# A hybrid encoder layer on one core: the seven sums of the second feed-forward product are combined to four blocks by VectorE as they are made, their operands are loaded by SyncE into four buffers, and the residual is kept in column chunks

## The chip, the core and the metric

One core of a Trainium2 chip runs the whole layer in one launch. The metric is the device time of that launch in microseconds (us). Three runs of the kernel before took 2177.72, 2178.38 and 2178.72 us; the median is 2178.38 us.

The engines have short names here: PE multiplies matrices, DVE (VectorE) does elementwise work on two tensors, ACT (ScalarE) does copies, casts and activations, POOL (GpSimd) and SP (SyncE) only issue DMAs in the part that matters. SBUF is the on-chip memory, PSUM the small memory that PE writes its sums to (eight banks of 128 x 512 floats), DRAM the memory off the core.

## What is computed

The input is 512 tokens of 2048 floats. The layer is a mixer (short convolutions beside gated linear attention), then a feed-forward block, each with a residual, and a last RMSNorm. Cut to what matters here:

```python
x = x + concat(y_conv, y_gla) @ w_out                 # 2048 x 2048
h = rmsnorm(x, norm2_g)
x = x + square(relu(h @ w_ff1)) @ w_ff2               # 2048 x 8192, 8192 x 2048
out = rmsnorm(x, norm_f_g)
```

## The kernel before

**Precision.** Every float operand of PE is split in two: `hi`, its value rounded to PE's format (a cast, done by ACT), and `lo`, the rest (a subtraction, done by DVE). A product is three matmuls, hi by hi, hi by lo, lo by hi. `split_w` (L602 to L607) does this for weights; it has three buffers for `hi` and three for `lo`, so that the operands of one product can be made only when the product three earlier is done. `plus` (L609 to L612) adds two weight blocks on DVE.

**Seven products in place of eight.** Both feed-forward products are done on 2 x 2 blocks by Winograd's form of Strassen's method: seven products of sums of blocks. Each is called by a number f (1 to 7), in the order `FORMS = (1, 5, 7, 3, 6, 2, 4)`. From the seven results come the four blocks of the output by seven additions.

**The first feed-forward product** (L615 to L670) makes, in 32 steps g, 256 rows of hidden values, squares them, and stores their seven sums ("forms") to DRAM in `a_keep`. The last two steps store plain blocks in `a_last`.

**The second product** (L681 to L791) is the part that changes. The 8192 hidden rows are cut in four blocks `blk` of two groups `grp`; the 2048 output columns in four column steps `n`. The loops run over blk, n, grp and f. A product is 24 matmuls of 256 columns per group (12 in group 1 of block 3, which is half as deep) and adds into a PSUM bank over the two groups. Names such as `lo_f_0113` say blk 0, n 1, grp 1, f 3. The weights come in quarters `raw_f` of 512 KB (four buffers, SP's queue, L598). Per product, ACT casts `hi_f` (L605) and DVE subtracts `lo_f` (L606); four of the seven also need a `plus` (L611).

The other operand, the forms of hidden values, is loaded in `form` (L683 to L696): seven per group, each 512 KB from `a_keep` into one of two buffers `st`, by a DMA that POOL issues (L688); then a cast `ah` (L694) and a subtraction `al` (L695). A group's forms stay for all four column steps. The next block's forms are made beside the products at the change from one block to the next: in (n, grp) = (3, 1) for group 0 and in (0, 0) for group 1.

When a product's second group is done, `evict` (L712 to L719) copies its bank by ACT to a tile `p` of 256 KB, which POOL stores to DRAM in `p_keep`; from block 1 on the DMA adds to what is there. In block 3 `combine(n)` (L721 to L744) loads the seven sums back by SP (L726), makes the four blocks with seven additions on DVE (L729), and adds them, scaled by the token's norm `r2`, to the residual tiles `x3t` with eight operations of 256 columns (L741). A last short stage multiplies the two plain groups and finishes the output (L838 to L867).

**The residual.** After the mixer, x is held in four tiles `xr` of 128 tokens by 2048. The output projection runs in five column chunks (`out_chunk`, L555; three of 512 columns, two of 256); each adds to its columns of `xr`. When all are done, four DMAs of 1024 KB store `xr` in `x_keep` (L575), from where block 3 loads it. The SBUF of these tiles is used again for the weights' sums `w` and the buffers `st`.

**What sets the order.** The functions are called in the order written, but a scheduler then orders the instructions of each engine by when it takes them to be ready. On the chip each engine keeps that order: what stands behind a waiting instruction waits too.

Of the kernel before, what the change touches and what calls it, by code (L numbers as in the profile page):

```python
# [14 lines left out]
P = 128  # L15
SEQ = 512
D = 2048
# [22 lines left out]
def hymba_kernel(  # L40
# [444 lines left out]
    p_keep = [[tc.dram_tile([P, 2, HALF], F32, name=f"p_keep{n}{f}") for f in FORMS] for n in range(4)]  # L485
# [3 lines left out]
    xs = [res.tile([P, D], F32, name=f"xr_{i}", tag=f"x{i}") for i in range(NT)]  # L489
    for i in range(NT):  # L490
        nc.gpsimd.dma_start(xs[i], x[i * P : (i + 1) * P, :])
# [28 lines left out]
    def h_block(kt, pool):  # L520
        b = bank(f"htr_{kt}", "aux")
        for i in range(NT):
            T.transpose(b[:, i * P : (i + 1) * P], xs[i][:, kt * P : (kt + 1) * P], ident)
# [29 lines left out]
    with tc.tile_pool(name="n2", bufs=1) as n2:  # L553

        def out_chunk(n, c, wsrc, w0, nunit, ncol, ktu, hook, ready=()):  # L555
# [10 lines left out]
        for n in range(3):  # L566
            at = {2: (2 * n - 2,), 5: (2 * n - 1,)} if n else {}
            out_chunk(n, slice(n * 512, (n + 1) * 512), w_out, 8 * n, 8, 512, 2, pairs_at(at), w_ready if n == 0 else ())
        for n in (3, 4):
            c = slice((n + 3) * HALF, (n + 4) * HALF)  # L570
            at = {0: (4,), 1: (5,), 2: (6,)} if n == 4 else {}
            out_chunk(n, c, w_out_tail, 4 * (n - 3), 4, HALF, 4, pairs_at(at))
        h_pair(7, n2)
        for i in range(NT):
            nc.gpsimd.dma_start(x_keep[i], xs[i])  # L575
# [98 lines left out]
    PLACE = {1: 0, 2: 1, 4: 2, 7: 3, 5: 4, 6: 5, 3: 6}  # L674
    first = [(hf, f"h{n}") for n in range(14)]
# [5 lines left out]
    with tc.tile_pool(name="ff", bufs=1, reuse_waits="tile") as ff:  # L681

        def form(blk, grp, f):  # L683

            n = FORMS.index(f)
            m = 2 if (blk, grp) == (3, 1) else 4
            raw = wt.tile([P, 4, HALF], F32, name=f"st_{blk}{grp}{f}", tag="st", bufs=2)
            nc.gpsimd.dma_start(raw[:, :m, :], a_keep[2 * blk + grp][PLACE[f]][:, :m, :])  # L688
# [23 lines left out]
        def evict(blk, n, f, dst):  # L712
            sq = ff.tile([P, 2, HALF], F32, name=f"p_{blk}{n}{f}", tag="sq", bufs=8)
            S.copy(sq, dst.rearrange("p (a b) -> p a b", a=2))  # L714
            keep = p_keep[n][FORMS.index(f)]
            if blk == 0:
                nc.gpsimd.dma_start(keep, sq)
            else:
                nc.gpsimd.dma_start(keep, sq, accum_op=ALU.add)  # L719

        def combine(n):  # L721

            s = {}
            for f in FORMS:
                s[f] = ff.tile([P, 2, HALF], F32, name=f"s_{n}{f}", tag="sq", bufs=8)
                nc.sync.dma_start(s[f], p_keep[n][FORMS.index(f)])  # L726

            def op(out, a, b, kind):
                V.tensor_tensor(out=s[out], in0=s[a], in1=s[b], op=kind)  # L729

            op(6, 6, 1, ALU.subtract)
            op(2, 1, 2, ALU.add)
            op(5, 5, 6, ALU.add)
            op(6, 6, 7, ALU.add)
            op(3, 5, 3, ALU.add)
            op(7, 5, 7, ALU.add)
            op(4, 4, 6, ALU.subtract)
            for f, row, col in ((3, 0, 0), (2, 0, 1), (7, 1, 0), (4, 1, 1)):
                for i in range(2):
                    xc = x3t[2 * row + i][col][:, n, :]  # L740
                    V.scalar_tensor_tensor(  # L741
                        out=xc, in0=s[f][:, i, :], scalar=r2[:, 2 * row + i : 2 * row + i + 1], in1=xc,
                        op0=ALU.mult, op1=ALU.add,
                    )  # L744
# [3 lines left out]
        for f in FORMS:  # L748
            form(0, 0, f)
        for blk in range(4):  # L750
            for n in range(4):
                dst = {f: fbank(f"f2_{blk}{n}{f}") for f in FORMS}
                for grp in range(2):
# [10 lines left out]
                    for f in FORMS:  # L764
                        if f == 5:
                            w = w1 = plus(b11, b12, m * HALF, f"{name}{f}")
                        elif f == 7:
                            w = plus(b11, b21, m * HALF, f"{name}{f}")
                        elif f == 6:
                            w = w3 = plus(w1, b21, m * HALF, f"{name}{f}")  # L770
                        elif f == 4:
                            w = plus(w3, b22, m * HALF, f"{name}{f}")
                        else:
                            w = {1: b12, 3: b21, 2: b22}[f]
                        product2(blk, grp, f, w, m, dst[f], f"{name}{f}")
                        if grp == 1:
                            evict(blk, n, f, dst[f])
# [4 lines left out]
                if blk == 3:  # L782
                    if n == 0:
                        x3t = []
                        for i in range(NT):
# [156 lines left out]
```

## Time and profile before

| | |
|---|---|
| median of three runs | 2178.38 us |
| the profiled execution | 2175.88 us, of which 2173.9 us span from first to last instruction |
| PE busy | 2089.0 us, 14408 matmuls |
| DVE busy | 1437.5 us |
| ACT busy | 933.8 us |
| POOL busy | 162.0 us |
| moved by DMA | 323.91 MB, 149 GB/s in the mean |

The profile divides the span by engine and instruction. A "group" is all instructions of a line with the same names and shapes; "idle before" is how long the engine stood before them, and for whom. A "wait" row names the waiting engine and who ended the wait. A row of "windows" gives, for a stretch of the span, each engine's busy time with its count of instructions (x), then the granted share of PE's clock (PEclk, 1.00 is full) and of DMA. PE's busy time is modelled and runs on over short pauses, so the count of matmuls in a stretch says more than the busy time. The first product ends at about 1434 us, the second at about 2114 us.

### The profile page before, as it was taken

What the parts mean: (1) busy time and instruction counts of PE and PEld (TensorE: products, weight loads), DVE (VectorE), ACT (ScalarE), POOL (GpSimd) and SP (SyncE); (2) the same over time, 40 slices, a digit from 0 to 9 for tenths busy, and PEclk for the clock granted to TensorE, in tenths of its full rate; (3) what the DMA queues carried; (4) which work ended last, traced back from release to release, by engine and by line L of the source; (5) the groups of instructions that cost most, each with busy time, mean ns of one, the idle gap of its engine ahead of it and who ended that gap; (6) DMA issues with size and microseconds to landing.
All of it is one profiled execution on the core that took longest, in us unless ns stands there. A gap on an engine that the chain in (4) does not pass through costs nothing.

```text
span 2173.9 us, 34501 instructions
## 1 busy us (share of the span) xinstructions
PE 2089.0 (96%) x14408; PEld 1935.0 (89%) x14408; DVE 1437.5 (66%) x1680; ACT 933.8 (43%) x1222; POOL 162.0 (7%) x233
## 2 busy tenths in 40 slices
PE   8999999999999989999999999999989989987887
PEld 7988877877888889999999999999989989987885
DVE  4232236656754488888888888887776676665666
ACT  6242212222333345555555555465454454453343
POOL 0000000000000000000000000011111121121120
PEclk9999999999999999999999999999999999999899
DMA  7223322222243344444445444566576786776574
GB/s 294 87 79 97 97 78 87 78 78 80 85 174 92 93 148 158 158 158 158 150 139 168 158 141 149 159 233 198 165 238 141 172 230 158 172 210 197 151 210 138
DMA packets 97532, 323.91 MB, mean 149 GB/s; under 512 B 10901, under 2 KB 10949, under 8 KB 95840
## 3 DMA queue, kind: packets, MB, share of 16 engines
q1 hardware_dynamic: 65088, 222.46, 32.0%
q0 software_dynamic: 32288, 99.24, 16.6%
q8 instruction: 113, 1.85, 0.3%
q14 instruction: 43, 0.35, 0.0%
HBM read 255.34 MB, written 66.32 MB: 148 GB/s over the span
## 4 chain that ended last, share of the span: by engine, by line
PE 73%; issue 15%; DMA 5%; DVE 3%; POOL 3%; ACT 1%; POOLq 0%; ACTq 0%; DVEq 0%; SPq 0%
PE f1c L625 8%; PE f1a L625 8%; PE f L707 8%; PE f1d L625 4%; PE f1e L625 4%; PE f1b L625 4%; DMA st<-a_keep 3%; PE tm_op L75 3%; PE tm_op L76 3%; PE tm_op L77 3%; POOL p_keep L719 2%; PE fm_ch L75 1%; PE fm_cc L75 1%; PE tm_v L76 1%; PE tm_v L75 1%
## 5 line engine op out<-in xcount | busy, mean ns | idle before, releaser
L707 PE MATMUL f<-lo_f,ah 128*128 128x256 f32 x1568 | 452.5, 289 | 43.4 <-DVE lo_f L606 43.4
L707 PE MATMUL f<-hi_f,ah 128*128 128x256 f32 x1568 | 446.9, 286 | 9.0 <-ACT hi_f L605 9.0
L707 PE MATMUL f<-hi_f,al 128*128 128x256 f32 x1568 | 447.1, 285 | 0.0
L606 DVE TENSOR_TENSOR lo_f<-w_f,hi_f 128x1024 fp32r<-128x1024 f32 (+1 forms) x256 | 304.4, 1190 | 149.6 <-ACT hi_f L605 148.3
L605 ACT CAST hi_f<-w_f 128x1024 fp32r<-128x1024 f32 (+1 forms) x256 | 262.0, 1023 | 241.5 <-PE f1c L625 97.0
L707 PEld LDWEIGHTS f<-lo_f,ah 128*128 128x128 f32 x1568 | 303.1, 193 | 50.0 <-DVE lo_f L606 49.9
L707 PEld LDWEIGHTS f<-hi_f,ah 128*128 128x128 f32 x1568 | 302.8, 193 | 10.5 <-ACT hi_f L605 10.4
L707 PEld LDWEIGHTS f<-hi_f,al 128*128 128x128 f32 x1568 | 303.9, 194 | 0.0
L605 ACT CAST hi_f<-raw_f 128x1024 fp32r<-128x1024 f32 (+1 forms) x192 | 196.6, 1024 | 192.1 <-PE f L707 82.9
L606 DVE TENSOR_TENSOR lo_f<-raw_f,hi_f 128x1024 fp32r<-128x1024 f32 (+1 forms) x192 | 227.6, 1186 | 20.9 <-ACT hi_f L605 20.7
L611 DVE TENSOR_TENSOR w_f<-raw_f,raw_f 128x1024 f32<-128x1024 f32 (+1 forms) x128 | 152.1, 1191 | 91.9 <-DMA raw_f<-in_w_ff 84.0
L611 DVE TENSOR_TENSOR w_f<-w_f,raw_f 128x1024 f32<-128x1024 f32 (+1 forms) x128 | 152.4, 1190 | 3.7
L625 PE MATMUL f1c<-Sh,hi_f 128*128 128x256 f32 x512 | 145.0, 283 | 6.2 <-ACT hi_f L605 6.2
L625 PE MATMUL f1c<-Sh,lo_f 128*128 128x256 f32 x512 | 144.9, 283 | 0.4 <-DVE lo_f L606 0.4
L625 PE MATMUL f1c<-Sl,hi_f 128*128 128x256 f32 x512 | 144.6, 282 | 0.0
L625 PE MATMUL f1a<-Sh,hi_f 128*128 128x256 f32 x512 | 144.2, 282 | 0.0
L625 PE MATMUL f1a<-Sh,lo_f 128*128 128x256 f32 x512 | 144.1, 282 | 0.0
L625 PE MATMUL f1a<-Sl,hi_f 128*128 128x256 f32 x512 | 144.0, 281 | 0.0
L75 PE MATMUL tm_op<-hi_op,yh 128*128 128x512 f32 (+1 forms) x304 | 106.2, 349 | 0.0
L714 ACT COPY p<-f 128x512 f32<-128x512 f32 x112 | 65.6, 586 | 92.9 <-PE f L707 92.9
L76 PE MATMUL tm_op<-lo_op,yh 128*128 128x512 f32 (+1 forms) x304 | 105.3, 346 | 0.0
L77 PE MATMUL tm_op<-hi_op,yl 128*128 128x512 f32 (+1 forms) x304 | 105.0, 345 | 0.0
(353 smaller groups left out, 4923.0 us busy)
## 6 DMA issues: line engine op xcount, KB each, us to landing
raw_f<-in_w_ff SPq DMA_DIRECT2D x240, 512.0 KB, 4.0
p_keep<-p POOLq DMA_DIRECT2D x112, 256.0 KB, 5.6
a_keep<-y POOLq DMA_DIRECT2D x30, 896.0 KB, 5.1
st<-a_keep POOLq DMA_DIRECT2D x49, 512.0 KB, 4.6
raw_op<-in_w_out SPq DMA_DIRECT2D x22, 512.0 KB, 3.6
raw_og<-in_w_feat SPq DMA_DIRECT2D x16, 512.0 KB, 3.7
raw_cc<-in_w_feat SPq DMA_DIRECT2D x16, 512.0 KB, 3.8
raw_ch<-in_w_feat SPq DMA_DIRECT2D x16, 512.0 KB, 3.7
```

The costliest lines, as they stand in the source:

```text
L75: T.matmul(dst, l[0], r[0], start=start, stop=False)
L76: T.matmul(dst, l[0], r[1], start=False, stop=False)
L77: T.matmul(dst, l[1], r[0], start=False, stop=stop)
L605: S.copy(hi[:, :n], src)
L606: V.tensor_tensor(out=lo[:, :n], in0=src, in1=hi[:, :n].bitcast(F32), op=ALU.subtract)
L611: V.tensor_tensor(out=w[:, :n], in0=in0, in1=in1, op=ALU.add)
L625: T.matmul(dst[:, :HALF], l[:, c], r, start=start and p == m == 0, stop=p == 7 and m == 2, skip_group_check=True,)
L707: T.matmul(d, l[:, k, t], r[:, c], start=grp == k == i == e == 0, stop=grp == 1 and k == m - 1 and e == 2, skip_group_check=True,)
L714: S.copy(sq, dst.rearrange("p (a b) -> p a b", a=2))
L719: nc.gpsimd.dma_start(keep, sq, accum_op=ALU.add)
```

## The change

1. **The sums stay on the chip.** `evict` no longer copies all seven banks out. Products run in the order `ORDER = (1, 6, 5, 3, 7, 2, 4)`. ACT copies only bank 1 (`q`); DVE reads the other banks and builds the four blocks by seven operations of 128 x 512 per column step (`t`, `x`, `v` and the blocks `c0` to `c3`), each reading one PSUM bank. Only the blocks go to DRAM, in `c_keep`: stored in block 0, added by the DMA in blocks 1 and 2. In block 3 the kept block `s` is loaded by POOL ahead of its step, added on DVE, and the result is added to `x3t` as before; `combine` is gone.
2. **Forms.** `st` is loaded by SP. Every second form of a full group takes one of two more buffers, slots `second[14]` and `second[15]`, which the first product uses up to its last matmuls for its forms 6, 2 and 4.
3. **Weights' sums.** In the new order the sums for f 5 and 6 are both made at f 6.
4. **The residual.** `xr` is 20 tiles, one per chunk and 128 tokens, loaded by 20 DMAs; each is stored in `x_keep` as soon as its chunk is added. The squares for the norm go to PSUM.

The diff, cut:

```diff
+    c_keep = [[tc.dram_tile([P, 2, HALF], F32, name=f"c_keep{n}{q}") for q in range(4)] for n in range(4)]
...
+    for n, c in enumerate(chunks):
+        for i in range(NT):
+            nc.gpsimd.dma_start(xs[n][i], x[i * P : (i + 1) * P, c])
...
             def put(i, b):
-                V.tensor_tensor(out=xs[i][:, c], in0=b[:, :ncol], in1=xs[i][:, c], op=ALU.add)
-                sq = n2.tile([P, 512], F32, name=f"sq2_{n}{i}", tag="sq2", bufs=1)
-                S.activation(sq[:, :ncol], xs[i][:, c], AF.Square, accum_out=ss2[:, i, n : n + 1])
+                xc = xs[n][i]
+                V.tensor_tensor(out=xc, in0=b[:, :ncol], in1=xc, op=ALU.add)
+                sq = bank(f"sq2_{n}{i}", "one")
+                S.activation(sq[:, :ncol], xc, AF.Square, accum_out=ss2[:, i, n : n + 1])
+                nc.gpsimd.dma_start(x_keep[i][:, chunks[n]], xc)
...
-        for i in range(NT):
-            nc.gpsimd.dma_start(x_keep[i], xs[i])
...
+    ORDER = (1, 6, 5, 3, 7, 2, 4)
...
-            raw = wt.tile([P, 4, HALF], F32, name=f"st_{blk}{grp}{f}", tag="st", bufs=2)
-            nc.gpsimd.dma_start(raw[:, :m, :], a_keep[2 * blk + grp][PLACE[f]][:, :m, :])
+            name = f"st_{blk}{grp}{f}"
+            if n % 2 and (blk, grp) != (3, 1):
+                raw = in_slot(second[14 + n // 2 % 2], name, F32)
+            else:
+                raw = wt.tile([P, 4, HALF], F32, name=name, tag="st", bufs=2)
+            nc.sync.dma_start(raw[:, :m, :], a_keep[2 * blk + grp][PLACE[f]][:, :m, :])
...
+        def evict(blk, n, f, dst, had):
+            p = dst[f].rearrange("p (a b) -> p a b", a=2)
+            def value(name, in0, in1, kind, bufs):
+                t = ff.tile([P, 2, HALF], F32, name=f"{name}_{blk}{n}", tag=name[0], bufs=bufs)
+                V.tensor_tensor(out=t, in0=in0, in1=in1, op=kind)
+                return t
+            def block(q, in0, in1, kind):
+                t = value(f"c{q}", in0, in1, kind, 4)
+                if blk == 0:
+                    nc.gpsimd.dma_start(c_keep[n][q], t)
+                elif blk < 3:
+                    nc.gpsimd.dma_start(c_keep[n][q], t, accum_op=ALU.add)
+                else:
+                    V.tensor_tensor(out=t, in0=t, in1=had["s"][q], op=ALU.add)
+                    for i in range(2):
+                        k = q // 2 * 2 + i
+                        xc = x3t[k][q % 2][:, n, :]
+                        V.scalar_tensor_tensor(
+                            out=xc, in0=t[:, i, :], scalar=r2[:, k : k + 1], in1=xc, op0=ALU.mult, op1=ALU.add
+                        )
+            if f == 1:
+                had["q"] = ff.tile([P, 2, HALF], F32, name=f"q_{blk}{n}", tag="q", bufs=1)
+                S.copy(had["q"], p)
+            if f == 6:
+                had["t"] = value("t", p, had["q"], ALU.subtract, 1)
+            if f == 5:
+                had["x"] = value("x", p, had["t"], ALU.add, 1)
+            if f == 3:
+                block(0, p, had["x"], ALU.add)
+            if f == 7:
+                had["v"] = value("v", p, had["t"], ALU.add, 1)
+                block(2, p, had["x"], ALU.add)
+            if f == 2:
+                block(1, p, had["q"], ALU.add)
+            if f == 4:
+                block(3, p, had["v"], ALU.subtract)
...
+                        if f == 6:
+                            w1 = plus(b11, b12, m * HALF, f"{name}5")
+                            w = w3 = plus(w1, b21, m * HALF, f"{name}6")
...
-                    combine(n)
```

Where the instructions stand now, at three places. **First**, DVE at the start of the first product. `w_f_05` is the first `plus` of its step 0, `lo_f_05` the split that its second product waits for; the rows ahead of them belong to the last pair of normed hidden inputs (`d_7`, `Sl`) and to the norm factor `r_`. Before:

```order
L577 TENSOR_REDUCE a_5708<-ss_4161 128x4
L544 TENSOR_TENSOR d_7_5700<-h_5680,d_7_5696 128x256
L531 TENSOR_TENSOR Sl_5665<-d_7_5692,Sh_5664 128x256
L531 TENSOR_TENSOR Sl_5667<-d_7_5696,Sh_5666 128x256
L531 TENSOR_TENSOR Sl_5665<-d_7_5700,Sh_5664 128x256
L118 TENSOR_SCALAR a_5708<-a_5708 128x4
L108 RECIPROCAL r_4162<-r_4162 128x4
```

In the row of before follow six more operations on the norm factor, then three `plus` (`w_f_05`, `w_f_07`, `w_f_06`), then `lo_f_05`. The same place now, with lines of the changed file:

```order
L582 TENSOR_REDUCE a_5744<-ss_4181 128x4
L616 TENSOR_TENSOR w_f_05_5812<-raw_f_01_5770,raw_f_00_5768 128x1024
L537 TENSOR_TENSOR Sl_5705<-d_7_5732,Sh_5704 128x256
L537 TENSOR_TENSOR Sl_5707<-d_7_5736,Sh_5706 128x256
L550 TENSOR_TENSOR d_7_5740<-h_5720,d_7_5736 128x256
L118 TENSOR_SCALAR a_5744<-a_5744 128x4
L616 TENSOR_TENSOR w_f_07_5844<-raw_f_01_5770,raw_f_02_5772 128x1024
L537 TENSOR_TENSOR Sl_5705<-d_7_5740,Sh_5704 128x256
L108 RECIPROCAL r_4182<-r_4182 128x4
L611 TENSOR_TENSOR lo_f_05_5815<-w_f_05_5812,hi_f_05_5814 128x1024
```

`w_f_05` moved up to right behind the reduction, and `lo_f_05` stands ahead of most of the norm's operations and of the third `plus`.

**Second**, a regular column step (blk 0, n 1, grp 1). Before, ACT alternates casts with the copies `p` of finished banks:

```order
L714 COPY p_14105<-f_011_13850 128x512
L605 CAST hi_f_0113_14174<-raw_f_0112_14073 128x1024
L714 COPY p_14138<-f_015_13851 128x512
L605 CAST hi_f_0116_14207<-w_f_0116_14205 128x1024
L714 COPY p_14171<-f_017_13852 128x512
L605 CAST hi_f_0112_14238<-raw_f_0113_14075 128x1024
```

Now DVE has the seven operations that read the banks (L728) between its splits and sums:

```order
L611 TENSOR_TENSOR lo_f_0113_14207<-raw_f_0112_14108,hi_f_0113_14206 128x1024
L728 TENSOR_TENSOR t_14174<-f_016_13886,q_14140 128x512
L611 TENSOR_TENSOR lo_f_0117_14240<-w_f_0117_14237,hi_f_0117_14239 128x1024
L728 TENSOR_TENSOR x_14204<-f_015_13887,t_14174 128x512
L616 TENSOR_TENSOR w_f_0206_14381<-w_f_0205_14379,raw_f_0202_14347 128x1024
L611 TENSOR_TENSOR lo_f_0112_14273<-raw_f_0113_14110,hi_f_0112_14272 128x1024
L728 TENSOR_TENSOR c_01_14234<-f_013_13888,x_14204 128x512
L611 TENSOR_TENSOR lo_f_0114_14306<-w_f_0114_14303,hi_f_0114_14305 128x1024
L616 TENSOR_TENSOR w_f_0207_14467<-raw_f_0201_14345,raw_f_0202_14347 128x1024
L728 TENSOR_TENSOR v_14267<-f_017_13889,t_14174 128x512
L728 TENSOR_TENSOR c_01_14269<-f_017_13889,x_14204 128x512
```

The operation on a bank stands behind the split of a product two further on, so that PE has work while DVE waits for the bank.

**Third**, DVE in block 3, from n 0 to n 1. Before, the additions of `combine(0)` stand inside the next step's first group, behind the split of its fourth product (`s` are the sums that came back from DRAM):

```order
L606 TENSOR_TENSOR lo_f_3107_19556<-w_f_3107_19553,hi_f_3107_19555 128x1024
L611 TENSOR_TENSOR w_f_3104_19669<-w_f_3106_19611,raw_f_3103_19493 128x1024
L606 TENSOR_TENSOR lo_f_3103_19584<-raw_f_3102_19491,hi_f_3103_19583 128x1024
L729 TENSOR_TENSOR s_19459<-s_19459,s_19451 128x512
L729 TENSOR_TENSOR s_19453<-s_19453,s_19459 128x512
```

Five more such additions and the eight operations of L741 follow there, then `lo_f_3106`. Now the last of the four blocks stands ahead of the next step's first split, and more behind it:

```order
L742 SCALAR_TENSOR_TENSOR x_01_19064<-c_30_19462,r_4182,x_01_19064 128x256
L742 SCALAR_TENSOR_TENSOR x_11_19068<-c_30_19462,r_4182,x_11_19068 128x256
L728 TENSOR_TENSOR c_30_19485<-f_304_19062,v_19439 128x512
L611 TENSOR_TENSOR lo_f_3101_19514<-raw_f_3100_19505,hi_f_3101_19513 128x1024
L738 TENSOR_TENSOR c_30_19485<-c_30_19485,s_19085 128x512
L616 TENSOR_TENSOR w_f_3106_19543<-w_f_3105_19541,raw_f_3102_19509 128x1024
L742 SCALAR_TENSOR_TENSOR x_21_19072<-c_30_19485,r_4182,x_21_19072 128x256
L742 SCALAR_TENSOR_TENSOR x_31_19076<-c_30_19485,r_4182,x_31_19076 128x256
L616 TENSOR_TENSOR w_f_3107_19629<-raw_f_3101_19507,raw_f_3102_19509 128x1024
L611 TENSOR_TENSOR lo_f_3106_19546<-w_f_3106_19543,hi_f_3106_19545 128x1024
```

The whole combining of step n is thus ahead of, or among, the first splits of step n + 1, in the row from `t` of step n on: `t`, `lo_f_3013`, `x`, `lo_f_3017`, `lo_f_3012`, `c0`, `lo_f_3014`, an addition L738, `v`, two operations L742, `c2`, `c1`, two additions, and then the rows shown.

More of the change, by code (lines that the diff above doesn't have):

```diff
@@ L484, in hymba_kernel @@
     a_last = tc.dram_tile([2, P, 4, HALF], F32, name="a_last")
-    p_keep = [[tc.dram_tile([P, 2, HALF], F32, name=f"p_keep{n}{f}") for f in FORMS] for n in range(4)]
+    c_keep = [[tc.dram_tile([P, 2, HALF], F32, name=f"c_keep{n}{q}") for q in range(4)] for n in range(4)]
     hf = ctx.enter_context(tc.tile_pool(name="hf", bufs=1))
@@ L488, in hymba_kernel @@
     res = late.enter_context(tc.tile_pool(name="res", bufs=1))
-    xs = [res.tile([P, D], F32, name=f"xr_{i}", tag=f"x{i}") for i in range(NT)]
-    for i in range(NT):
-        nc.gpsimd.dma_start(xs[i], x[i * P : (i + 1) * P, :])
+    chunks = [slice(0, 512), slice(512, 1024), slice(1024, 1536), slice(1536, 1792), slice(1792, 2048)]
+    xs = [
+        [res.tile([P, c.stop - c.start], F32, name=f"xr_{n}{i}", tag=f"x{n}{i}") for i in range(NT)]
+        for n, c in enumerate(chunks)
+    ]
+    for n, c in enumerate(chunks):
+        for i in range(NT):
+            nc.gpsimd.dma_start(xs[n][i], x[i * P : (i + 1) * P, c])
     ss2 = const_tile("ss2", [P, NT, 5])
@@ L710, in product2 @@
                         )
[L712 to L744, printed above, removed]
@@ L746, in hymba_kernel @@
         aforms = {}
         x3t = None
-        for f in FORMS:
+        for f in ORDER:
             form(0, 0, f)
@@ L751, in hymba_kernel @@
             for n in range(4):
-                dst = {f: fbank(f"f2_{blk}{n}{f}") for f in FORMS}
+                dst = {f: fbank(f"f2_{blk}{n}{f}") for f in ORDER}
+                had = {}
+                if blk == 3:
+                    if n == 0:
+                        x3t = []
+                        for i in range(NT):
+                            x3t.append([in_slot(second[7 + 2 * i + c], f"x3_{i}{c}", F32) for c in range(2)])
+                            for c in range(2):
+                                nc.gpsimd.dma_start(
+                                    x3t[i][c], x_keep[i][:, c * 1024 : (c + 1) * 1024].rearrange("p (a b) -> p a b", a=4)
+                                )
+                    had["s"] = []
+                    for q in range(4):
+                        had["s"].append(ff.tile([P, 2, HALF], F32, name=f"s_{n}{q}", tag="s", bufs=4))
+                        nc.gpsimd.dma_start(had["s"][q], c_keep[n][q])
                 for grp in range(2):
@@ L781, in hymba_kernel @@
                             form(blk + 1, 0, f)
[L782 to L785, printed above, removed]
-                            x3t.append([in_slot(second[7 + 2 * i + c], f"x3_{i}{c}", F32) for c in range(2)])
-                            for c in range(2):
-                                nc.gpsimd.dma_start(
-                                    x3t[i][c], x_keep[i][:, c * 1024 : (c + 1) * 1024].rearrange("p (a b) -> p a b", a=4)
-                                )
-                    combine(n)
         slots = first + second[:7]
@@ L849, in hymba_kernel @@
                 )
-                sq = ff.tile([P, 512], F32, name=f"sq3_{n}{i}", tag="sq", bufs=8)
-                S.activation(sq, x3[n], AF.Square, accum_out=ss3[:, i, n : n + 1])
+                sq = ff.tile([P, 2, HALF], F32, name=f"sq3_{n}{i}", tag="c", bufs=4)
+                S.activation(sq.rearrange("p a b -> p (a b)"), x3[n], AF.Square, accum_out=ss3[:, i, n : n + 1])
                 if n < 3:
```

27 lines of the change are left out of this document (11 added, 16 removed).

## The prediction

> **What bounds the kernel now.** I read the page's busy shares first, then the groups of instructions with the idle time ahead of them. From the page:
>
> ```profile
> span 2173.9 us, 34501 instructions
> L707 PE MATMUL f<-lo_f,ah 128*128 128x256 f32 x1568 | 452.5, 289 | 43.4 <-DVE lo_f L606 43.4
> L606 DVE TENSOR_TENSOR lo_f<-w_f,hi_f 128x1024 fp32r<-128x1024 f32 (+1 forms) x256 | 304.4, 1190 | 149.6 <-ACT hi_f L605 148.3
> L714 ACT COPY p<-f 128x512 f32<-128x512 f32 x112 | 65.6, 586 | 92.9 <-PE f L707 92.9
> ```
>
> PE bounds nearly all of it; in the second product it stands before a matmul almost only for a split `lo_f`. A share over the span does not say where, so the third view is the table by windows, cut at the start of the first product, the start of the second, a regular part, the changes of block, the steps of block 3, and the last stage:
>
> ```profile
> core 0: us, PE busy (x) PEld busy (x) DVE busy (x) ACT busy (x) POOL busy (x), PEclk, DMA share, GB/s
> 789.30:800.50 11.20, 4.31 (x17) 3.64 (x17) 10.76 (x23) 4.65 (x8) 0.00 (x0) 0.70 0.84 318
> 1434.00:1480.00 46.00, 41.08 (x339) 40.05 (x338) 39.25 (x35) 29.31 (x35) 9.64 (x18) 1.00 0.77 262
> 1579.00:1630.00 51.00, 44.23 (x340) 43.01 (x339) 38.82 (x34) 28.29 (x32) 9.15 (x17) 0.93 0.71 235
> 1749.00:1820.00 71.00, 63.70 (x509) 61.90 (x508) 51.85 (x45) 38.15 (x45) 16.71 (x23) 0.98 0.81 212
> 1820.00:1919.00 99.00, 99.00 (x840) 98.89 (x840) 69.50 (x58) 46.74 (x53) 15.07 (x19) 1.00 0.67 168
> 1919.00:1988.50 69.50, 57.33 (x423) 54.99 (x422) 40.19 (x43) 32.34 (x45) 19.48 (x28) 0.93 0.75 204
> 1988.50:2032.00 43.50, 33.37 (x254) 32.57 (x253) 27.51 (x38) 14.97 (x21) 6.02 (x7) 0.88 0.63 165
> 2032.00:2075.00 43.00, 33.31 (x255) 32.51 (x254) 28.20 (x38) 14.98 (x21) 6.02 (x7) 0.91 0.63 167
> 2075.00:2114.20 39.20, 33.43 (x254) 32.82 (x254) 29.10 (x39) 17.51 (x24) 6.27 (x8) 0.89 0.70 200
> ```
>
> The row 1820:1919 sets the scale: PE without a pause, 99.00 / 840 = 0.1179 us a matmul, so 24 x 0.1179 = 2.83 us a product and 19.8 us a group of seven. In the other rows the excess is the width less the count times 0.1179: 46.00 - 40.0 = 6.0; 51.00 - 40.1 = 10.9; 71.00 - 60.0 = 11.0; 69.50 - 49.9 = 19.6; block 3: 125.7 - 763 x 0.1179 = 35.7; and at the first product 11.20 - 2.0 = 9.2. Together some 92 us, the most that this change could free. A regular column step has no excess: what is made cheaper there is worth nothing.
>
> **Start of the first product: -2.3.** PE and DVE there, each in its timeline:
>
> ```profile
> 795.54 0.58 PE L625 MATMUL f1c<-Sh,hi_f 128*128 128x256 f32 x1 [6.16 <-ACT hi_f L605]
> 797.87 0.58 PE L625 MATMUL f1c<-Sh,lo_f 128*128 128x256 f32 x1 [0.39 <-DVE lo_f L606]
> ```
>
> ```profile
> 790.12 0.17 DVE L577 TENSOR_REDUCE a<-ss 128x4 f32<-128x20 f32 x1
> 793.18 2.36 DVE L611 TENSOR_TENSOR w_f<-raw_f,raw_f 128x1024 f32<-128x1024 f32 x2
> 796.60 2.35 DVE L606 TENSOR_TENSOR lo_f<-w_f,hi_f 128x1024 fp32r<-128x1024 f32 x2
> ```
>
> PE's second product waits for the cast of `w_f_05`, then for `lo_f_05`. `w_f_05` now stands right behind the reduction, near 790.3 and not 793.18; its split follows cast, two more operations of 1.2 us and a few small ones later, near 794.3 and not 796.60. The gain is 2.3, at most 4 if the cast is the only thing left between, 0 if the early `plus` now waits for its tile.
>
> **Start of the second product: 0.** The forms load four at a time and not two, which alone would free most of the 6.0. But form 6 now is the second product, and its new buffer is held by the last matmuls of the first product. What a form costs is in the rows of DMA issues and, for cast and split, in the groups of a regular stretch (1480 to 1579):
>
> ```profile
> raw_f<-in_w_ff SPq DMA_DIRECT2D x240, 512.0 KB, 4.0
> st<-a_keep POOLq DMA_DIRECT2D x49, 512.0 KB, 4.6
> ...
> x<-x_keep POOLq DMA_DIRECT2D x8, 512.0 KB, 9.4
> ```
>
> ```profile
> L606 DVE TENSOR_TENSOR lo_f<-w_f,hi_f 128x1024 fp32r<-128x1024 f32 x20 | 24.5, 1224 | 16.6 <-ACT hi_f L605 16.6
> L605 ACT CAST hi_f<-w_f 128x1024 fp32r<-128x1024 f32 x19 | 19.9, 1049 | 14.3 <-PE f L707 14.3
> ```
>
> Load 4.6 + cast 1.05 + split 1.22 - 2.83 of product 1 = 4.0 us of pause, and a pause like that lowers the clock, some 1.7 more: 5.7 against 6.0. I take 0; -4 if the matmuls that hold the slot end early, +3 if the load is late behind the first weights on SP's queue.
>
> **Regular column steps: 0.** Per step DVE gains seven operations on banks. The nearest rows are an addition from PSUM in the mixer (L423) and the same addition from SBUF (L729):
>
> ```profile
> L423 DVE TENSOR_TENSOR up<-fm_ch,cc 128x512 f32<-128x512 f32 x8 | 5.5, 692 | 20.3 <-PE fm_ch L77 20.3
> L729 DVE TENSOR_TENSOR s<-s,s 128x512 f32<-128x512 f32 x28 | 17.7, 686 | 14.7 <-DMA s<-p_keep 14.6
> L741 DVE SCALAR_TENSOR_TENSOR x<-s,r,x 128x256 f32<-128x256 f32 x32 | 13.1, 476 | 0.0
> ```
>
> A step is 22 operations of 1.22 and seven of 0.69: 31.7 of 39.6 us. It fits, and an operation on a bank stands behind the split of a product two further on, so PE has 2 x 2.83 us in hand. ACT loses six of seven copies of 0.59, off the path. SP's queue is passed by forms only at the change of block. If weights landed 6 us after issue rather than 4.0, a step would lose about 0.5: up to +6 over twelve steps.
>
> By the 692 ns and the 686 ns above, reading a bank costs 6 ns more than reading SBUF. [...]
>
> **Changes of block 0 to 1 and 1 to 2: -8.9 and -9.0.** Waits of 1579 to 1630, each row us in total, times, longest:
>
> ```profile
> ACT ah L694 <- DMA st<-a_keep: 19.1, 7, 5.5
> POOL st L688 <- DVE al L695: 19.1, 8, 6.6
> ...
> PE f L707 <- DVE lo_f L606: 4.2, 5, 1.6
> ```
>
> POOL can issue a form only when an earlier one is split; ACT then waits for it with the weights' casts queued behind; DVE's split and PE follow. With four buffers a load has three forms' time, 3 x 2.83 = 8.5 us, against 4.6 + 1.05 + 1.22 = 6.9: the stall goes. What is late next is DVE. From the group (3, 1) on it has some 40 operations of 1.2 and seven of 0.65 per 18 products, 52.6 against 50.9 us, a deficit of 1.7, in part covered by the buffers of `lo`. I leave 2 of each excess (0 to 6).
>
> **Change 2 to 3: -14.6.** Here the second group's forms are short, 256 KB, and still have two buffers; the eight loads of `x_keep`, 9.4 us each, come in a burst on POOL's queue. Both remain, and the four loads of `s` join them, but no form stands behind them on POOL now. I leave 5 of 19.6 (1 to 12).
>
> **Steps of block 3: -5.** Waits of 1988.5 to 2114, and the combining of step 0 in DVE's timeline:
>
> ```profile
> PE f L707 <- DVE lo_f L606: 22.0, 8, 7.3
> DVE s L729 <- DMA s<-p_keep: 14.3, 4, 6.1
> ```
>
> ```profile
> 2000.91 4.42 DVE L729 TENSOR_TENSOR s<-s,s 128x512 f32<-128x512 f32 x7 [6.06 <-DMA s<-p_keep]
> 2005.26 3.25 DVE L741 SCALAR_TENSOR_TENSOR x<-s,r,x 128x256 f32<-128x256 f32 x8
> 2008.43 1.22 DVE L606 TENSOR_TENSOR lo_f<-w_f,hi_f 128x1024 fp32r<-128x1024 f32 x1
> ```
>
> DVE waits 6.06 for the way through DRAM, works 7.5 on the combining, and the split that PE needs stands behind. The wait goes. The work stays and grows: seven bank operations, four additions L738 and eight L742. In the short group, whose seven products take 9.9 us, `t` can start at about 3; behind it, up to `lo_f_3101`, come 14 operations at 4.42 / 7 = 0.63 (four of them short splits), six at 3.25 / 8 = 0.41 and the split's 1.14: 12.4 us. That ends at 15.4: PE idles 15.4 - 9.9 = 5.5 us. The split of the second product, `lo_f_3106`, stands 4.9 us behind (0.63 + 1.13 + 0.81 + 1.13 + 1.22), 2.1 more than a product. With about 0.6 for the clock beyond what that covers: 8.2, three times 24.6. At the last step the chain delays the fourth product's split by about 5.8. Together 30.4 of 35.7 remain.
>
> The clock after such pauses, PE alone:
>
> ```profile
> core 0: us, PE busy (x), PEclk, DMA share, GB/s
> 1605.00:1618.00 13.00, 9.58 (x56) 0.74 0.69 246
> 2000.00:2018.00 18.00, 9.80 (x59) 0.72 0.33 94
> ```
>
> [...]
>
> **Last stage: +1.5**, for half clock behind the last step's pause. The stores of the residual by chunk lie beside PE's work in the output projection; 0, within 1 either way, since the four stores before had landed long before they were read.
>
> **Sum.** -2.3 - 8.9 - 9.0 - 14.6 - 5.3 + 1.5 = -38.6. The profiled execution's own 2175.9 (2173.9 of span, 2.0 around it) becomes 2137.3. The median stands 2.5 above it and becomes 2178.4 - 38.6 = **2140**. A measurement here can tell about 0.2%, 4.4 us.
>
> **Rivals.** *Forms still late.* A form on SP's queue waits there for its buffer, and the weights behind it wait too, which POOL's queue did not do. For it: ACT's 19.1 us of waiting is for landings, at a DMA share of 0.71 to 0.81 that does not fall. Against: buffers a load longer. Then two thirds of 8.9 + 9.0 + 14.6 stay, 2140 + 22 = 2162. *DVE keeps up everywhere*, block 3 too, if its splits run ahead of the combining: some 75 of the 92 us go, 2103. Against: the order shown, with `c_3` ahead of `lo_f_3101`. *Slower: bank operations take DVE's time.* Each stands in DVE's fixed row and waits for a finished product, with splits behind it. Should one cost 1.2 us rather than 0.69, a column step has 26.8 + 8.4 = 35 of 39.6 us, little enough that one bank's wait can hold a split for about a product, 3 us, in each of twelve steps: 36. At three changes of block the load is 56.4 against 50.9, 3.8 more each: 11. In three steps of block 3 the chain grows by 7 x 0.5: 11. Together 2140 + 58 = 2198. It decides from about 1.0 us. Against: 692 ns from PSUM. [...] *The change does nothing*: the loss moves whole to DVE, 2178.
>
> **How the numbers follow.** Forecast 0.62; forms late 0.16; DVE keeps up 0.10; no change 0.04; slower 0.08. The forecast's own ends are its terms' ends taken together in part, 2122 to 2155. To leave out at most 2 in 10 the range takes in the late forms with their spread, and some of the freer cases: 2112 to 2168. Faster 0.88, within 0.2% 0.04, slower 0.08.
>
> **What would show it.** Right: bank operations at about 0.69; no pause over 1.5 us at the changes 0 to 1 and 1 to 2, and ACT's waits for `st` there under 6 us in all; excess of 5 at 2 to 3; in block 3 three pauses of 5 to 6 ahead of the first product of a step, for `lo_f_3n01`; in the first product the wait for `lo_f_05` ends near 795.6 in place of 797.87. Wrong: `raw_f` landing late behind forms on SP (weights' sums waiting for DMA); pauses in the regular steps; block 3 without pauses.

## The result and the profile after

The changed kernel took 2128.39 us in the median of four runs (2126.53 to 2130.57), against 2178.05 before (2173.09 to 2178.72): a ratio of 0.978, 95% interval 0.976 to 0.980. It is 50 us faster; 39 were forecast. The profiled execution took 2126.53, with a span of 2124.8. From its page:

```profile
span 2124.8 us, 34341 instructions
L717 PE MATMUL f<-lo_f,ah 128*128 128x256 f32 x1568 | 446.7, 285 | 20.2 <-DVE lo_f L611 20.2
L717 PE MATMUL f<-hi_f,ah 128*128 128x256 f32 x1568 | 443.3, 283 | 8.2 <-ACT ah L704 4.9
```

PE's idle time ahead of matmuls that need a `lo_f` has fallen from 43.4 us to 20.2, and 4.9 us of waiting for a form's cast stand out. Where the time went is read best from PE's own records: the first matmul of each group (blk, n, grp), and from one to the next. "No pause" is the count of matmuls by 0.1179 us. The table has one trace of each kernel; how far such a stretch moves from trace to trace is said below where it matters.

| stretch, us | no pause | before | after | forecast for the difference | measured |
|---|---|---|---|---|---|
| start of the kernel to first matmul of the second product | | 1433.99 | 1431.21 | -2.3 | -2.8 |
| its first two groups | 39.6 | 46.00 | 46.28 | 0 | +0.3 |
| (0,1,0) to (1,1,0): change 0 to 1 | 158.6 | 169.75 | 158.55 | -8.9 | -11.2 |
| (1,1,0) to (2,1,0): change 1 to 2 | 158.6 | 170.08 | 161.57 | -9.0 | -8.5 |
| (2,1,0) to (3,1,0): change 2 to 3 | 148.6 | 168.69 | 158.24 | -14.6 | -10.5 |
| (3,1,0) to (3,3,1): block 3 | 79.3 | 115.05 | 101.52 | -11.1 | -13.5 |
| (3,3,1) to the end: last short group, last stage | | 70.38 | 67.45 | +7.3 | -2.9 |
| sum | | 2173.94 | 2124.82 | -38.6 | -49.1 |

(The forecast's 35.7 to 30.4 for block 3 is split here as it was worked out: 24.6 left in the three steps, 5.8 at the last step, to which the 1.5 of the last stage is added.) The table by windows of the changed kernel, the same places as before:

```profile
core 0: us, PE busy (x) PEld busy (x) DVE busy (x) ACT busy (x) POOL busy (x), PEclk, DMA share, GB/s
1431.20:1477.50 46.30, 41.44 (x339) 41.23 (x338) 42.42 (x41) 25.88 (x28) 2.18 (x4) 0.96 0.79 267
1576.60:1636.00 59.40, 59.40 (x506) 59.40 (x505) 55.61 (x56) 30.64 (x31) 3.94 (x6) 1.00 0.66 215
1817.40:1916.50 99.10, 99.10 (x842) 99.10 (x841) 84.85 (x83) 45.38 (x47) 11.37 (x15) 1.00 0.60 159
1896.70:1955.85 59.15, 52.42 (x423) 51.40 (x421) 44.51 (x56) 23.36 (x30) 8.40 (x13) 0.97 0.74 223
1955.85:1993.00 37.15, 32.12 (x254) 31.71 (x253) 29.77 (x42) 12.07 (x15) 2.16 (x4) 0.91 0.39 114
1993.00:2030.30 37.30, 32.28 (x255) 31.86 (x253) 29.87 (x42) 12.08 (x15) 2.15 (x4) 0.91 0.41 115
```

The second row holds the change 0 to 1: PE does 506 matmuls in 59.4 us without a pause, while DVE is busy for 55.6 of them. ACT's waits for a form to land, 19.1 us before, are down to this over 1576 to 1636:

```profile
ACT ah L704 <- DMA st<-a_keep: 2.2, 2, 1.6
```

The third row of the table runs up to the end of block 2. It is at full rate as before, although DVE now does 84.9 us of work there, not 69.5. The last two rows are steps of block 3: 29.8 us of DVE's work in 37 us, and PE at a clock of 0.91. Why they are not 29.7 us long shows in DVE's timeline from one step to the next, with PE's record of the wait under it:

```profile
1956.36 1.28 DVE L738 TENSOR_TENSOR c<-c,s 128x512 f32<-128x512 f32 x2
1957.56 1.66 DVE L742 SCALAR_TENSOR_TENSOR x<-c,r,x 128x256 f32<-128x256 f32 x4
1959.14 0.68 DVE L728 TENSOR_TENSOR c<-f,v 128x512 f32<-128x512 f32 x1
1959.74 1.21 DVE L611 TENSOR_TENSOR lo_f<-raw_f,hi_f 128x1024 fp32r<-128x1024 f32 x1
```

```profile
1961.01 0.58 PE L717 MATMUL f<-lo_f,ah 128*128 128x256 f32 x1 [4.88 <-DVE lo_f L611]
```

DVE waits for nothing there. The split that PE needs stands behind additions that nobody waits for; 5.5 us of pause were forecast, 4.9 came. The last stage in DVE's timelines, of before and then of the changed kernel, first the place of the additions (before only), then the end of the program:

```profile
2130.32 1.96 DVE L729 TENSOR_TENSOR s<-s,s 128x512 f32<-128x512 f32 x3 [0.30 <-DMA s<-p_keep]
2132.19 0.48 DVE L741 SCALAR_TENSOR_TENSOR x<-s,r,x 128x256 f32<-128x256 f32 x1
2132.59 2.49 DVE L729 TENSOR_TENSOR s<-s,s 128x512 f32<-128x512 f32 x4
2135.00 2.85 DVE L741 SCALAR_TENSOR_TENSOR x<-s,r,x 128x256 f32<-128x256 f32 x7
...
2164.12 0.75 DVE L847 SCALAR_TENSOR_TENSOR x<-e,r,x 128x512 f32<-128x512 f32 x1
```

```profile
2115.83 0.75 DVE L867 SCALAR_TENSOR_TENSOR x<-e,r,x 128x512 f32<-128x512 f32 x1 [0.43 <-PE e L77]
```

The last matmuls start at 2160.37 and at 2115.40. Before, DVE came to the last bank 3.75 us after the last matmul began: 7.5 us of combining, from 2130.32 to 2137.85, lay in this stage. Now it waits for PE. What I had not read ahead of the prediction is this: the last step's combining was in the last stage.

### The profile page after: what moved, and what is told of

Read it like the earlier page. It is cut to its first block, busy times and chain, and to the rows that moved or that the text cites. A ratio compares the mean times of both kernels' runs of the same rounds, so it can differ in the third digit from the quotient of the medians.

```text
span 2124.8 us, 34341 instructions
## 1 busy us (share of the span) xinstructions
PE 2073.0 (98%) x14408; PEld 1925.0 (91%) x14408; DVE 1491.6 (70%) x1780; ACT 887.9 (42%) x1126; POOL 106.3 (5%) x161
## 4 chain that ended last, share of the span: by engine, by line
PE 91%; DVE 4%; DMA 2%; issue 1%; ACT 1%; ACTq 0%; DVEq 0%; POOLq 0%
PE f L717 23%; PE f1c L630 9%; PE f1a L630 8%; PE f1d L630 4%; PE f1e L630 4%; PE f1b L630 4%; PE tm_op L75 3%; PE tm_op L76 3%; PE tm_op L77 3%; PE fm_ch L75 2%; PE fm_cc L75 2%; PE tm_v L76 1%; PE tm_v L75 1%; PE tm_v L77 1%; PE fm_og L77 1%; PE fm_cb L76 1%
## 5 line engine op out<-in xcount | busy, mean ns | idle before, releaser
L717 PE MATMUL f<-lo_f,ah 128*128 128x256 f32 x1568 | 446.7, 285 | 20.2 <-DVE lo_f L611 20.2
L616 DVE TENSOR_TENSOR w_f<-raw_f,raw_f 128x1024 f32<-128x1024 f32 (+1 forms) x128 | 152.3, 1190 | 42.0 <-DMA raw_f<-in_w_ff 39.6
L630 PEld LDWEIGHTS f1c<-Sh,hi_f 128*128 128x128 f32 x512 | 97.4, 190 | 3.4 <-ACT hi_f L610 3.4
```

The lines of the kernel that those rows point to most:

```text
L616: V.tensor_tensor(out=w[:, :n], in0=in0, in1=in1, op=ALU.add)
L630: T.matmul(dst[:, :HALF], l[:, c], r, start=start and p == m == 0, stop=p == 7 and m == 2, skip_group_check=True,)
L717: T.matmul(d, l[:, k, t], r[:, c], start=grp == k == i == e == 0, stop=grp == 1 and k == m - 1 and e == 2, skip_group_check=True,)
```

## Experiments

Times are medians; each run's before, on the same chip, lay between 2174.98 and 2178.84 us. "Stretch" is a row of the table above.

**Which part frees the change of block: buffers, queue, or the sums.** Theory: with two buffers a form can load only when an earlier one is split. Rival: the queue, or the traffic of the seven sums. Two buffers on SyncE's queue:

```diff
-            if n % 2 and (blk, grp) != (3, 1):
-                raw = in_slot(second[14 + n // 2 % 2], name, F32)
-            else:
-                raw = wt.tile([P, 4, HALF], F32, name=name, tag="st", bufs=2)
+            raw = wt.tile([P, 4, HALF], F32, name=name, tag="st", bufs=2)
```

> The changed kernel with two form buffers in place of four, still loaded by SyncE. Theory (buffers): a form can load only when an earlier one is split, so the changes of block 0 to 1 and 1 to 2 lose some 8 to 10 us each again and 2 to 3 a few more: 2148 us, 2142 to 2160. Rival (the 20 MB less of DMA traffic, or the queue, freed the changes of block): 2126 to 2132.

Four buffers on GpSimd's queue:

```diff
-            nc.sync.dma_start(raw[:, :m, :], a_keep[2 * blk + grp][PLACE[f]][:, :m, :])
+            nc.gpsimd.dma_start(raw[:, :m, :], a_keep[2 * blk + grp][PLACE[f]][:, :m, :])
```

> The changed kernel with its four form buffers, the loads issued by GpSimd as before the change. Theory (buffers): 2125 to 2133, no change, since a load has 8.5 us of time and the stores ahead of it on that queue wait for operations of VectorE that are done in time. Rival (the queue matters: forms stand behind stores of blocks that wait for VectorE): some 5 us at each change of block, 2140 to 2150.

Both edits together:

> Two form buffers and GpSimd's queue, everything else of the changed kernel. Theory (buffers): like two buffers on SyncE, 2148, within 5 us of that run. Rival (queue): more than that run by 10 us or over.

And the kernel before with the four buffers and SyncE's queue alone (the first diff the other way round, `nc.sync` for `nc.gpsimd`):

> The kernel before with four form buffers loaded by SyncE and nothing else of the change. Theory (buffers): the two full changes of block lose their 10.9 and 11.0 us and 2 to 3 some 4: 2178 - 24 = 2154, 2148 to 2162. Rival (the seven sums that go to DRAM by accumulating stores hold up the loads): 2170 to 2180.

| us | total | first two groups | change 0 to 1 | 1 to 2 | 2 to 3 | first and last split of block 1's 14 forms done |
|---|---|---|---|---|---|---|
| no pause | | 39.6 | 158.6 | 158.6 | 148.6 | |
| before (two, GpSimd, seven sums) | 2178 | 46.0 | 169.8 | 170.1 | 168.7 | 1565 to 1620 |
| changed, two, GpSimd | 2148.53 | 50.1 | 164.1 | 168.2 | 162.1 | 1568 to 1625 |
| changed, two, SyncE | 2131.55 | 44.0 | 161.2 | 162.8 | 159.2 | 1562 to 1616 |
| changed, four, GpSimd | 2137.57 | 51.1 | 158.9 | 162.7 | 161.5 | 1568 to 1616 |
| changed | 2128.39 | 46.3 | 158.6 | 161.6 | 158.2 | 1563 to 1610 |
| before, four, SyncE | 2142.28 | 44.2 | 158.7 | 161.5 | 157.0 | 1564 to 1601 |

My theory failed in the first run and held for the rest only in part. Two buffers on SyncE's queue, at 2131.55, lie in the rival's range: they cost 2.7 us at the first change where I expected 8 to 10. Both edits together are 17 us slower than that, which was the rival's condition, so the queue counts; only there does the loss come near what I expected, 5.6 and 6.6 us. Four buffers on GpSimd's queue, at 2137.57, lie between theory and rival: of the 9 us, 4.8 are at the start of the second product and 3.3 at the change 2 to 3. In the changed kernel either of the two edits, more buffers or the other queue, thus frees most of the changes 0 to 1 and 1 to 2, and they do not add up.

That the loads need the sums' traffic out of the way is refuted. The kernel before, which still sends all seven to DRAM, has the changed kernel's times at the changes of block once its forms have the four buffers on SyncE's queue; it even falls below the theory's range, since the change 2 to 3 gave 12 us, not 4. That part alone is worth 34 of the 50 us. The rest of the change frees part of the same loss, though: with two buffers on GpSimd's queue the changed kernel is still 27 us faster than before, and takes 5.6, 1.9 and 6.6 us less at the three changes. Whether the fewer stores on that queue or the other order of the products does this was not tested. Block 3 is the clear case: its stretch is 114.6 us with the buffers and queue alone and 100.5 with all but them, so its gain comes from the rest of the change, with which the way of the sums through DRAM is gone.

Waits at the change 0 to 1 with two buffers, on SyncE and then on GpSimd (us in total, times, longest):

```profile
ACT ah L701 <- DMA st<-a_keep: 16.9, 9, 3.9
PE f L714 <- DVE lo_f L611: 1.3, 3, 0.7
```

```profile
POOL st L695 <- DVE al L702: 34.4, 9, 5.7
ACT ah L701 <- DMA st<-a_keep: 17.2, 8, 3.4
PE f L714 <- DVE lo_f L611: 2.6, 3, 1.7
```

ACT waits for landings for as long in both, 17 us, about the 19.1 of before; PE's waits for splits are 1.3 and 2.6 us. So a wait of 19 us on ACT was not in itself the loss that I took it for. With two buffers the 14 forms of a block take 54 to 57 us on either queue, with four 37 to 48. Much the same pace costs PE 2.7 us on one queue and 5.6 on the other, and the difference has two parts. On SyncE's queue PE's pauses there were 0.72 and 0.40 us and the granted clock stayed at 1.00. On GpSimd's they were 1.71 and 0.59, and after the first of them the clock was 0.55 for 2.5 us and 0.88 for the next 5 (the rows are in the last section). Why the pause is longer there is not settled: the forms share their turn with the stores of the blocks, and the copy `q` and some casts stand at other places of ACT's row, and these runs do not part the two. The start of the second product is 5 to 6 us longer with GpSimd's queue in both cases.

**Block 3: DVE's order, or DVE's time.** The additions are collected and written behind products of the next step:

```diff
-                    V.tensor_tensor(out=t, in0=t, in1=had["s"][q], op=ALU.add)
...
+                    def add():
+                        V.tensor_tensor(out=t, in0=t, in1=had["s"][q], op=ALU.add)
...
+                    if n < 3:
+                        late_ops.append(add)
+                    else:
+                        add()
...
+                        elif late_ops and f in (5, 3, 7, 2):
+                            late_ops.pop(0)()
```

> The changed kernel; in block 3 the four additions of the kept blocks and the eight scaled additions of steps 0 to 2 are written behind products 3 to 6 of the next step's first group, not behind their own product. Theory (DVE's order delays the next step's first split; DVE as such has room: 28.9 us of work in 29.7 us of PE's): each of three steps of 37.2 us falls to 31 to 33, 2128 - 15 = 2113, 2107 to 2119. Rival (DVE is the bound in block 3): the pauses come back at later products, 2124 to 2130.

Measured: 2115.89 (2112.77 to 2116.72), ratio to before 0.971 (0.969 to 0.973). The steps fell from 37.2 to 32.1 us, as the theory said; the last stretch grew from 67.5 to 70.7. DVE at the same place, and a whole step:

```profile
1957.03 0.69 DVE L730 TENSOR_TENSOR c<-f,q 128x512 f32<-128x512 f32 x1
1957.64 1.22 DVE L611 TENSOR_TENSOR lo_f<-raw_f,hi_f 128x1024 fp32r<-128x1024 f32 x1
1958.77 0.68 DVE L730 TENSOR_TENSOR c<-f,v 128x512 f32<-128x512 f32 x1
```

```profile
core 0: us, PE busy (x) PEld busy (x) DVE busy (x) ACT busy (x) POOL busy (x), PEclk, DMA share, GB/s
1952.00:1984.00 32.00, 30.91 (x254) 30.07 (x253) 29.52 (x42) 11.78 (x15) 2.17 (x4) 1.00 0.40 133
```

The same 29.5 us of DVE's work now fill 32 us. Nothing was taken away; the split moved ahead, and without a long pause the clock was 1.00 where it had been 0.91: the pauses at the steps are 4.9 us long in the changed kernel, and the longest here is 0.8 us. The clock also fell, to 0.55, behind the pause of 1.71 us above.

**The last stage.** The kernel before without its last combining:

```diff
-                    combine(n)
+                    if n < 3:
+                        combine(n)
```

> The kernel before; the combining of the last column step (its seven loads, seven additions and eight scaled additions) is left out, so 256 columns of each half lack the second product. Theory (in the last stage of before, VectorE does this work beside the last splits and additions, and PE and the end of the kernel wait for it): the stage from the last short group on takes 70.4 - 5 = 65.4 us, 2176 - 5 = 2171, 2168 to 2173. Rival (the last stage is set by the loads of its weights and by PE): 2175 to 2178.

The last stretch took 66.9 us, not 70.4 (nor 70.2, as in the kernel before with four buffers, whose last stage is the same): 3.5 of the 5 expected. In the total, 2173.51 (2169.59 to 2176.08) against 2175.14, this is inside the spread (ratio 0.998 to 1.000); the trace alone shows it. Its DVE reaches the last bank at 2161.70, after a last matmul at 2160.63, without the lag of before. Then the later additions once more, with the last step's too, each ahead of the tile of the last stage that needs it:

```diff
-                    if n < 3:
-                        late_ops.append(add)
-                    else:
-                        add()
+                    late_ops.append(add)
...
+                if late_ops and n in (2, 1):
+                    late_ops.pop({(0, 2): 0, (0, 1): 1, (1, 2): 0, (1, 1): 0}[i, n])()
```

> The kernel that writes block 3's additions later, and in addition those of the last column step inside the last stage, each ahead of the first tile that needs it (the squares there go to the one buffer of another tile). Theory (in the last stage too, only the place of this work in VectorE's order costs): that stage falls from the 70.7 us of the run before to 65 or 66, 2116 - 5 = 2111, 2108 to 2114. Rival (VectorE as such is the bound there): 2114 to 2119.

2108.71 (2106.72 to 2112.81), ratio 0.969 (0.968 to 0.971), the fastest here: 20 us below the changed kernel by the medians, 18 by the spans of the profiled executions (2107.0 against 2124.8). The last stretch is 65.2 us, as expected.

**Whether the operations on banks take DVE's time.** Each is done twice in blocks 0 to 2:

```diff
-                V.tensor_tensor(out=t, in0=in0, in1=in1, op=kind)
+                for _ in range(2 if blk < 3 else 1):
+                    V.tensor_tensor(out=t, in0=in0, in1=in1, op=kind)
```

> The changed kernel; in blocks 0 to 2 every one of the seven operations of a column step on VectorE that reads a PSUM bank is done twice. Theory (they have room: 31.7 + 4.3 = 36 of 39.6 us): 0 in the regular column steps, 2 to 4 us at each of three changes of block, where the forms' splits lie too: 2128 + 9 = 2137, 2131 to 2143. Rival (an operation that waits for a bank holds up the splits behind it, so a second one costs PE its 0.6 us each time or up to 3 us a step): 2128 + 36 = 2164, over 2150.

2141.10 (2139.39 to 2142.31), inside the theory's range: the first steps of blocks 1 and 2 took 4.2 and 2.3 us longer, and the third change lost nothing. The regular steps lost up to 1.8 us each where I had said 0, always at a step's first product. DVE there, with PE's wait:

```profile
1518.99 0.69 DVE L729 TENSOR_TENSOR c<-f,x 128x512 f32<-128x512 f32 x1
1519.59 0.69 DVE L729 TENSOR_TENSOR c<-f,q 128x512 f32<-128x512 f32 x1
1520.19 1.23 DVE L611 TENSOR_TENSOR lo_f<-raw_f,hi_f 128x1024 fp32r<-128x1024 f32 x1
```

```profile
1521.47 0.39 PE L717 MATMUL f<-lo_f,ah 128*128 128x256 f32 x1 [0.74 <-DVE lo_f L611]
```

The room in a regular step is thus less than the 7.9 us that 31.7 of 39.6 suggests: at a step's end five operations come together, and what counts is how far ahead of PE the next split then is. The rival of 3 us a step is out.

**Three that gave nothing.** Form 6 in a buffer of the old pair:

```diff
-            if n % 2 and (blk, grp) != (3, 1):
-                raw = in_slot(second[14 + n // 2 % 2], name, F32)
+            if n // 2 % 2 and (blk, grp) != (3, 1):
+                raw = in_slot(second[14 + n % 2], name, F32)
```

> The changed kernel; the two extra buffers take the third and fourth form (and the seventh), so that form 6, of the second product, loads early into a buffer of the old pair. Theory (the pause of 5.1 us at the second product is form 6 waiting for its slot): 2128 - 5 = 2123, 2120 to 2125. Rival (form 5, now in the slot, comes as late and stops the third product, with the weights behind it on SyncE's queue): 2126 to 2131.

2126.04 (2125.93 to 2132.26), and the first two groups took 47.8 us, not less: the pause moved from the second product to the third (2.45 and then 1.39 us there). The rival was right. The residual loaded back by column step:

```diff
+                    for i in range(NT):
+                        for c in range(2):
+                            at = c * 1024 + n * HALF
+                            nc.gpsimd.dma_start(x3t[i][c][:, n, :], x_keep[i][:, at : at + HALF])
```

> The changed kernel; the residual is loaded back in block 3 by column step (8 DMAs of 128 KB behind the kept blocks of each step) in place of 8 DMAs of 512 KB at once. Theory (what is left at the change 2 to 3, some 9 us, is the burst of 4 MB that delays the forms: landings of 6.7 us at a DMA share near 1): 2128 - 5 = 2123, 2119 to 2126. Rival (the short forms' two buffers are what is left): 2127 to 2131.

and a third buffer for the short forms:

```diff
+            elif (blk, grp) == (3, 1) and n % 3 == 2:
+                raw = in_slot(second[15], name, F32)
```

> The changed kernel; the short forms of the last group take a third buffer (the slot that the residual does not use). Theory (what is left at the change 2 to 3 is ACT waiting for short forms, with casts behind, because only two can load at a time): 158.2 us of this stretch become 154, 2128 - 4 = 2124, 2120 to 2127. Rival (the DMA engines are full there, so a third load only shares them): 2127 to 2131.

2129.47 and 2128.63; the change 2 to 3 took 161.7 and 159.8 us against 158.2. Both guesses at what is left there failed. The waits of 1896 to 1956, of the changed kernel and of these two in turn:

```profile
ACT a L704 <- DMA st<-a_keep: 19.9, 6, 9.1
PE f L717 <- ACT hi_f L610: 3.3, 1, 3.3
```

```profile
ACT a L704 <- DMA st<-a_keep: 20.4, 5, 9.9
```

```profile
ACT a L706 <- DMA st<-a_keep: 14.5, 4, 8.6
```

ACT still waits for one short form for 9 us, with casts behind it, and PE for one of these casts. The rows of the changed kernel show what that form waited for. Its load goes into the buffer of an earlier short form, whose cast ACT had done at 1904.4, but whose split stands in DVE's row behind seven other operations. SyncE issues the load as that split ends, and it lands 8 us later, at a DMA share of 0.98 over 1913 to 1921:

```profile
1912.31 0.68 DVE L705 TENSOR_TENSOR a<-st,a 128x512 fp32r<-128x512 f32 x1
1913.02 0.33 SPq L698 DMA_DIRECT2D st<-a_keep  x1
1921.21 0.62 ACT L704 CAST a<-st 128x512 fp32r<-128x512 f32 x1 [9.09 <-DMA st<-a_keep]
```

In the other two kernels it is the same: a split of DVE ends at 1914.25 and at 1912.48, and the load follows at 1914.28 and at 1912.50. The third buffer only moved the wait to the next form. So here too the place of an operation in DVE's row seems to hold things up; a run with these splits written earlier was not made.

**The residual whole again**, four tiles and four loads and stores:

```diff
+    whole = [res.tile([P, D], F32, name=f"xr_{i}", tag=f"x{i}") for i in range(NT)]
...
-                nc.gpsimd.dma_start(x_keep[i][:, chunks[n]], xc)
...
+            nc.gpsimd.dma_start(x_keep[i], whole[i])
```

> The changed kernel with the residual in four tiles of 1 MB again, loaded by four DMAs and stored by four when all columns are done. Theory (the first weights' sums of the first product wait for the tiles' space, which the chunks free early): the first product starts 2.8 us later, 2131, 2129 to 2134. Rival (it came from the order of the operations alone): 2127 to 2129.

In the trace the second product starts 3.2 us later, at 1434.38, and `w_f_05` is made where it was before:

```profile
793.38 1.23 DVE L614 TENSOR_TENSOR w_f<-raw_f,raw_f 128x1024 f32<-128x1024 f32 x1
```

The total, 2127.69 (2124.43 to 2129.49), shows nothing of it; 3 us are inside the spread of runs. The traces do: in the ten of kernels with chunks the second product starts at 1430.9 to 1432.8, in the four with whole tiles at 1434.0 to 1434.8. Space freed early and operations reordered come together in this edit, so the runs do not tell which of them moves the start.

## Why the prediction was right, and where it was not

- **Start of the first product, -2.3**: -2.8, by the row that it named; PE's second product began at 792.50 in place of 795.54, and the first matmul with `lo_f_05` came at 795.36, where 795.6 was forecast.
- **Start of the second, 0**: +0.3. The pause is form 6's, 4.9 us where 4.0 were worked out. The 1.7 for the clock was an estimate of mine that no row showed; 1.8 us were lost besides the pause, with a clock of 0.56 over 1439 to 1442 us and of 0.95 over 1442 to 1450.
- **Regular steps, 0**: 0. Bank operations took the time forecast from the mixer's row:

```profile
L728 DVE TENSOR_TENSOR c<-f,x 128x512 f32<-128x512 f32 x32 | 21.8, 681 | 0.0
L738 DVE TENSOR_TENSOR c<-c,s 128x512 f32<-128x512 f32 x16 | 10.6, 681 | 0.0
```

 An operation with one operand in a bank and one with both in SBUF cost the same 681 ns.
- **Changes of block, -8.9 and -9.0**: -11.2 and -8.5. The sizes were right, the reason was one of two. "With four buffers the stall goes" is true: ACT's waits for `st` are 2.2 us and, at the change 1 to 2, 5.0, both under the 6 named as a sign. But with SyncE's queue two buffers would nearly have done. At the change 1 to 2 a pause of 2.0 us came, where none over 1.5 was to be; this stretch took 158.5 to 161.6 us in five traces of kernels that are alike up to there, so it counts for little.
- **Change 2 to 3, -14.6**: -10.5; 9.6 us stay, not 5, inside the 1 to 12 given. The forecast put them down to the two buffers and the burst of `x_keep`; the rows of the experiments point to a late split in DVE's row.
- **Block 3's three steps**: 24.6 us of loss forecast, 22.3 measured, from the cause that was named; moving the additions alone took 5 us out of each step. The parts lay a little otherwise. The pause was 4.9 us, not 5.5, and the second wait, for `lo_f_3106` (2.1), did not show; the rest of the loss, 2.7 us a step, went with a clock of 0.91 over the step and 0.50 over 1961 to 1965 us, where 0.6, an estimate that no row showed, were given for the clock. That 2.1 and 0.6 make the same sum is luck.
- **Last step and last stage, +5.8 and +1.5**: -2.9. This is the term that failed, by 10 us, about the whole miss of 10.5; the errors of the other terms cancel. It went wrong twice.
 First, PE. Up to the start of the last matmul this stretch took 58.0 us, only 1.2 more than the 56.8 of before (56.9 to 58.9 in nine traces with this last stage). The longest of its pauses was 1.7 us, ahead of the seventh product, where one of 5.8 ahead of the fourth was forecast:

```profile
2073.14 0.38 PE L717 MATMUL f<-lo_f,a 128*128 128x256 f32 x1 [1.70 <-DVE lo_f L611]
```

 PE did not stand idle for the whole delay: 14 of the last stage's matmuls, at 0.227 us 3.2 us of work, ran ahead of that product. With the last step's additions moved too, this part is 55.8 us, so their place cost some 2.2 us, not 7.3.
 Second, the end. The clock was taken to be the only thing that the last stage would feel. Half clock is in the trace of before, 0.50 over 2009.7 to 2014 us behind the pause of 7.29 us, but no run shows the 1.5 us that were put on this stage for it: in the changed kernel the clock was 1.00 from 2074.5 to 2115.6 us. And before, that stage held the last combining on DVE, and DVE ended late: from the last matmul on, 13.6 us became 9.4. Leaving that combining out of before takes 3.5 us off the stretch, 3.2 of them here. PE did not wait for it: its two pauses in that stage, of 0.76 us each, came ahead of the combining and stay without it.
- The rivals: late forms (2162), bank operations that take DVE's time (2198) and a loss that moves whole to DVE did not come. DVE's keeping up everywhere (2103) did not come by itself, but the last kernel, at 2109, comes near it with another order alone.

## What to carry to other kernels

When an engine's row is a fixed order, ask of each operation ahead of a wanted one whether anybody waits for it; the same work in another order was worth 18 to 20 us here, more than a third of what the whole change brought. Count the stage that comes after the changed one too: work that leaves a loop's last step may have been lying in the next stage. And two remedies for one stall should be tried each alone, since either may be nearly all of it.

## What the runs showed of the hardware that was not expected

An issue of a form of 512 KB took 0.53 us on GpSimd and 0.32 us on SyncE's queue, in the timelines of the two runs with two buffers:

```profile
1576.18 0.53 POOL L695 DMA_DIRECT2D st<-a_keep  x1 [4.91 <-DVE al L702]
```

```profile
1596.53 0.32 SPq L695 DMA_DIRECT2D st<-a_keep  x1
```

After the pause of 4.9 us in block 3 the granted clock was 0.80 over 1955 to 1972 us; in the same window of the run with later additions, which has no such pause, it was 1.00 and PE did 130 matmuls, not 87. It also fell behind a much shorter pause: in the run with two buffers on GpSimd's queue it was 0.55 behind one of 1.71 us that ended at 1592.52. In the prediction's row 1605 to 1618 of before, at 0.74, the longest pause is 2.54 us. It did not fall behind the pause of 1.99 us at the changed kernel's change 1 to 2, where it was 1.00 over 1792 to 1800 us. The rows of the changed kernel, of the later additions, and of the two buffers:

```profile
core 0: us, PE busy (x), PEclk, DMA share, GB/s
1955.00:1972.00 17.00, 12.12 (x87) 0.80 0.44 123
...
1955.00:1972.00 17.00, 16.05 (x130) 1.00 0.42 142
...
1592.50:1595.00 2.50, 2.48 (x12) 0.55 0.84 247
1595.00:1600.00 5.00, 5.00 (x40) 0.88 0.64 203
```
